# Another order of steps in a hybrid layer of gated DeltaNet and sparse attention

## The chip, the cores and the metric

The kernel runs on one core of one Trainium2 chip. The metric is the device time of one execution in microseconds (us). Before the change the median of three runs is 738.63 us (738.37 to 744.95).

## What is computed

One layer over 1024 tokens of 1024 numbers, in float32. A modulation of the input's root-mean-square norm gives `h`; one product `h @ w_in` (3792 columns) gives everything that follows, for two groups of heads. In outline:

```
h    = rmsnorm(x, g_pre) * (1 + scale) + shift           # shift, scale, gate from silu(c) @ w_ada
qkv, z_a, b, a, q_b, ckv, z_b, iq, ik, iw = split(h @ w_in)
# group A: 4 heads of 128, chunks of 64 tokens
q, k, v = silu(causal_conv(qkv, width 4)), q and k to length 1
T    = inverse(I + strict_lower((k beta) k^T decay))      # per head and chunk, 64 x 64
u, w = T (v beta), T (k beta exp(gc))
v'   = u - w S;  o = (q exp(gc)) S + ((q k^T) decay) v';  S = S exp(g_last) + k^T v'   # chunk after chunk
o_a  = rmsnorm(o, g_gdn) * silu(z_a)
# group B: 4 heads of 128 over a shared latent
score = sum over 8 index heads of iw * relu(iq ik^T), causal
sel   = the 256 highest scores of each query
o_b   = softmax(q_b ckv[sel]^T + bias) ckv[sel] w_uv * silu(z_b)
out  = x + gate * rmsnorm([o_a, o_b] @ w_out, g_post)
```

## The kernel before, in words

Products in float32 precision are made of three matmuls of split operands: the high part of a weight times both parts of `h`, and its low part times the high part of `h` (L430 to L432). A tile of 128 weight columns needs two halves of 24 such matmuls of 512 tokens each. Weight tiles come through a pipeline of one raw and two split buffers: each use (`nextw`) splits the next raw tile into `whi` (L174 or L176) and `wlo` (L181) and starts the load of the one after (L233, on SP's queue). The projections' results take turns in two PSUM banks, so the second next half waits until a half has been read.

What runs when comes from three tables. `PLAN` (L37) is a list of step names; each name is a generator that issues its instructions up to its next `yield`. `PARTS` says how many steps each has, and `ENGINES` (L59) puts single instructions on another engine than the usual one. A scheduler then orders what each engine gets, and weighs it by the steps' order. On the chip every engine takes its instructions in the order that results.

The steps which the change and the prediction speak of:

- `F`, `D0`, `D1`, `X`, `E`: first halves of projections, the input's norm and transposes, group A's decays' inputs.
- `I`, twelve steps: index queries, three steps for each of four weight tiles, and the scores of two heads each. A score is relu on ACT (L590), then either one DVE instruction (L189) or a multiply on ACT (L192) and an add on POOL (L193). The matmuls of scores are L579 and L580. `S`, twenty steps: the search for the 256th highest score bit by bit, by counts on ACT (L619) and DVE (L607); a round closes with L659 and L660.
- `K0`, `K1`: keys of a pair of heads with their convolutions (`conv_half`, L705; each tap is one `add_scaled`, L186 to L193), decay matrices (L537), and the stores of the matrices to invert (L850).
- `J0`, `J1`: the inverses' 32-wide blocks (`invert`). A load of `scr` (L861), a memset (L862), then thirty rounds of one multiply (L867) and one add (L869), all on POOL; a store (L871) and eight loads of `X` (L876).
- `M0`, `M1` (`merge`): transposes of `X` on DVE (L919, L920), then matmuls which put the blocks together. `R0`, `R1`: the recurrence. `Q`, `V`: queries and values with convolutions; `Z0`, `Z1`: group A's gates; `N`, `A`: its norm and mix.
- `HZ`, four steps: gates of group B. Each is one weight tile, silu on ACT (L1029) and a store (L1031). `HQ`: its queries (L1145 stores them).
- `C`: latents; `G`: the residual gate (its weights are loaded at L1055); `B`: biases; `W`: loads of `w_out`; `T0` to `T7`: attention of a block of 128 queries; `O0` to `O7`: the output product of a block.

The inverse's chain and its load and store:

```python
ns = blk((64, 32, 32), name="ns")
nc.sync.dma_start(flat(ns), scr[pr, 0])                 # L861
for i in range(30, 0, -1):
    G.tensor_tensor(tmp, ns[..i..], ns[..i+1..], op=ALU.mult)       # L867
    G.tensor_tensor(ns[..], ns[..], tmp, op=ALU.add)                # L869
    yield
nc.sync.dma_start(scr[pr, 1], flat(ns))                 # L871
```

`blk` takes the free buffer with the lowest number, so a step placed earlier may get another buffer, and waits for its last reader.

Of the kernel before, what the change touches and what calls it, by code (L numbers as in the profile page):

```python
# [36 lines left out]
PLAN = ("D0 F F X X X D1 F I F E I I K0 K0 I I I K0 I I K0 I I I I K0 HZ J0 J0 J0 J0 J0 J0 J0 J0 J0 J0 J0 J0 J0 "  # L37
# [4 lines left out]
        "O2 O7 O7 O5 O2").split()  # L42
# [7 lines left out]
for _p in range(8):  # L50
# [8 lines left out]
ENGINES = {"ad00": "V", "ad01": "V", "ad20": "V", "ad30": "V", "ad50": "V", "cT0": "V", "cT1": "V", "cv011": "A",  # L59
# [53 lines left out]
def hybrid_kernel(ctx, tc, x, c, w_ada, b_ada, g_pre, conv_w, a_log, dt_bias, g_gdn, g_kv, w_uv,  # L113
# [53 lines left out]
    def engine(site, usual, choice):  # L167
        SITES[site] = usual, choice
        return ENGINES.get(site, usual)

# [51 lines left out]
    readers = [1, 5]  # L222
    for n in PLAN:
        if done[n] in PARTS[n][1]:
# [1106 lines left out]
    step = dict.fromkeys(PARTS, 0)  # L1331
    outs = [n for n in PLAN if n[0] == "O"]
    for pos, n in enumerate(PLAN):
        if n == "B":
# [48 lines left out]
```

## Time and profile before

| | |
|---|---|
| median of three runs | 738.63 us |
| profiled execution | 746.19 us, span 744.5 us, mean granted TensorE clock 0.964 |
| TensorE matmul busy | 685.7 us (92%) |
| DVE / ACT / POOL busy | 529.7 / 436.9 / 336.3 us |
| DMA | 70.10 MB, mean 94 GB/s |

The granted clock is in shares of the full one. A matmul that waits shows in its row what released it, as `[0.57 <-DVE score L189]`: idle 0.57 us, ended by DVE's instruction that wrote `score` at line 189. SPq is SP's queue of DMA issues, `ps` a PSUM bank. Names like `ps` stand for many buffers.

### The profile page before, as it was taken

To read this page: it belongs to the slowest core of one execution; us is meant where nothing else is said; L and a number is where in the kernel's file an instruction comes from. 1 tells how busy PE (TensorE), PEld (TensorE's weight loads), DVE (VectorE), ACT (ScalarE), POOL (GpSimd) and SP (SyncE) were. 2 spreads that over 40 slices of the span, in tenths; PEclk is the share of its full clock that TensorE was granted. 3 is DMA by queue.
4 is the path that set the end of the run, shared out by engine and by line. 5 is a ranking of instruction groups with operands and counts; after the bars stand their busy time and mean duration, and the time that the engine had idled before them with its cause. 6 is when DMAs were issued, how large, how long until landed. Compare 5 with 4: busy or idle time off the path is not lost.

```text
span 744.5 us, 11292 instructions
## 1 busy us (share of the span) xinstructions
PE 685.7 (92%) x3863; PEld 574.7 (77%) x3863; DVE 529.7 (71%) x1342; ACT 436.9 (59%) x863; POOL 336.3 (45%) x395
## 2 busy tenths in 40 slices
PE   3999898999999899998998999988887999999996
PEld 2887787888778678876787878777765889888885
DVE  3977785663356866868689887877889999964212
ACT  4545584576668888859868494523336687434211
POOL 2146616456997300314432599941243232654310
PEclk9996999999999999999999999996799999999999
DMA  8931000013112111220032212276033205313311
GB/s 309 405 153 44 1 29 28 1 40 104 42 47 96 43 68 47 90 81 29 1 114 113 86 57 86 71 250 235 15 115 114 85 29 185 114 61 124 141 58 56
DMA packets 35287, 70.10 MB, mean 94 GB/s; under 512 B 11431, under 2 KB 18717, under 8 KB 35230
## 3 DMA queue, kind: packets, MB, share of 16 engines
q1 hardware_dynamic: 35230, 69.39, 26.5%
q8 instruction: 30, 0.49, 0.3%
q14 instruction: 27, 0.22, 0.1%
HBM read 53.64 MB, written 15.73 MB: 93 GB/s over the span
## 4 chain that ended last, share of the span: by engine, by line
PE 54%; DVE 16%; POOL 11%; DMA 6%; ACT 6%; issue 5%; SPq 1%; DVEq 0%; POOLq 0%; ACTq 0%
PE ps L430 8%; PE ps L432 8%; PE ps L431 8%; PE ps L1281 4%; PE ps L1279 4%; PE ps L1280 4%; POOL ns L869 4%; POOL rk L867 4%; ACT junk L619 2%; DVE pr L1217 1%; PE ps L1234 1%; DMA wraw<-in_w_tiles_dram 1%; DMA wa<-in_w_ada_dram 1%; DVE junk L607 1%; PE ps L579 1%
## 5 line engine op out<-in xcount | busy, mean ns | idle before, releaser
L430 PE MATMUL ps<-h,whi 128*128 128x512 f32 (+2 forms) x448 | 177.2, 396 | 12.8 <-DVE cv L189 6.7
L431 PE MATMUL ps<-h,whi 128*128 128x512 f32 (+2 forms) x448 | 177.0, 395 | 0.0
L432 PE MATMUL ps<-h,wlo 128*128 128x512 f32 (+2 forms) x448 | 176.0, 393 | 0.7 <-POOL wlo L181 0.7
L619 ACT ACTIVATE junk<-score,pat,sgn 128x1024 bf16<-128x1024 f32 (+2 forms) x93 | 105.5, 1135 | 11.5 <-DVE pat L660 10.3
L430 PEld LDWEIGHTS ps<-h,whi 128*128 128x128 f32 (+1 forms) x448 | 85.5, 191 | 34.2 <-DVE cv L189 7.8
L432 PEld LDWEIGHTS ps<-h,wlo 128*128 128x128 f32 (+1 forms) x448 | 85.4, 191 | 17.3 <-issue 0.9
L431 PEld LDWEIGHTS ps<-h,whi 128*128 128x128 f32 (+1 forms) x448 | 85.4, 191 | 15.9 <-issue 0.7
L607 DVE TENSOR_SCALAR_CACHE_REDUCE junk<-score,pat 128x640 bf16<-128x640 f32 (+2 forms) x93 | 68.8, 740 | 1.6
L193 POOL TENSOR_TENSOR cv<-cv,tmp 128x510 f32<-128x510 f32 (+2 forms) x33 | 39.1, 1186 | 42.6 <-ACT tmp L192 42.3
L1281 PE MATMUL ps<-woh,ml 128*128 128x512 f32 x128 | 49.9, 392 | 1.3 <-DVE ml L181 1.3
L590 ACT ACTIVATE ps<-ps 128x512 f32<-128x512 f32 (+3 forms) x70 | 34.1, 511 | 28.5 <-PE ps L580 27.9
L1280 PE MATMUL ps<-wol,mh 128*128 128x512 f32 x128 | 50.4, 394 | 0.0
L1279 PE MATMUL ps<-woh,mh 128*128 128x512 f32 x128 | 50.0, 393 | 0.0
L193 POOL TENSOR_TENSOR score<-score,tmp 128x512 f32<-128x512 f32 (+3 forms) x29 | 32.4, 1123 | 35.0 <-ACT tmp L192 30.7
L189 DVE SCALAR_TENSOR_TENSOR score<-ps,iw,score 128x384 f32<-128x384 f32 (+3 forms) x41 | 25.7, 643 | 28.1 <-ACT ps L590 22.8
L869 POOL TENSOR_TENSOR ns<-ns,rk 64x30 f32<-64x30 f32 (+14 forms) x60 | 36.1, 602 | 3.8
L181 POOL TENSOR_TENSOR wlo<-wraw,whi 128x1024 fp32r<-128x1024 f32 (+1 forms) x11 | 25.7, 2340 | 26.7 <-PE ps L432 19.9
L867 POOL TENSOR_TENSOR rk<-ns 64x30 f32<-64x30 f32 (+14 forms) x60 | 36.2, 604 | 3.2
L189 DVE SCALAR_TENSOR_TENSOR cv<-ps,cols,cv 128x511 f32<-128x511 f32 (+2 forms) x39 | 28.8, 738 | 6.2 <-POOL cv L193 4.3
L174 ACT ACTIVATE whi<-wraw 128x1024 fp32r<-128x1024 f32 x19 | 20.0, 1054 | 20.1 <-PE ps L431 12.7
L1283 ACT ACTIVATE junk<-ps 128x512 bf16<-128x512 f32 x16 | 9.5, 595 | 36.8 <-PE ps L1281 32.3
L181 DVE TENSOR_TENSOR wlo<-wraw,whi 128x1024 fp32r<-128x1024 f32 x19 | 24.7, 1299 | 8.7 <-ACT whi L174 7.8
(358 smaller groups left out, 1742.1 us busy)
## 6 DMA issues: line engine op xcount, KB each, us to landing
wraw<-in_w_tiles_dram SPq DMA_DIRECT2D x29, 512.0 KB, 3.5
wa<-in_ada_tiles_dram SPq DMA_DIRECT2D x16, 512.0 KB, 10.2
x<-in_x_dram SPq DMA_DIRECT2D x8, 512.0 KB, 3.3
qd<-qo SPq DMA_DIRECT2D x8, 512.0 KB, 3.0
wa<-in_w_ada_dram SPq DMA_DIRECT2D x8, 512.0 KB, 5.1
qb<-qd SPq DMA_DIRECT2D x8, 512.0 KB, 3.2
woraw<-in_w_out_dram SPq DMA_DIRECT2D x8, 512.0 KB, 3.4
xr<-in_x_dram SPq DMA_DIRECT2D x8, 512.0 KB, 3.9
```

Source lines behind the costliest of these rows:

```text
L189: V.scalar_tensor_tensor(o, a, scale, o, op0=ALU.mult, op1=ALU.add)
L193: G.tensor_tensor(o, o, tmp, op=ALU.add)
L430: mm(o, lhsT=hi[:, k, :], rhs=h[:, 0, c0:c1], start=(k == 0), stop=False)
L431: mm(o, lhsT=hi[:, k, :], rhs=h[:, 1, c0:c1], start=False, stop=False)
L432: mm(o, lhsT=lo[:, k, :], rhs=h[:, 0, c0:c1], start=False, stop=(k == NK - 1))
L607: V.tensor_scalar(junk[:, 0:src.shape[1]], src, t, None, op0=op, op1=ALU.add, accum_out=o)
L619: A.activation(junk[:, 0:(b + 1) * P], score[b], AF.Sign, scale=sg, bias=t, accum_out=o)
L867: G.tensor_tensor(tmp, ns[:, 0:i, i:i + 1].to_broadcast([64, i, w]), ns[:, i:i + 1, i + 1:32].to_broadcast([64, i, w]), op=ALU.mult)
L869: G.tensor_tensor(ns[:, 0:i, i + 1:32], ns[:, 0:i, i + 1:32], tmp, op=ALU.add)
L1279: mm(ps, lhsT=mh[:, k, :], rhs=woh[k][:, sl], start=(k == 0), stop=False)
L1280: mm(ps, lhsT=mh[:, k, :], rhs=wol[k][:, sl], start=False, stop=False)
L1281: mm(ps, lhsT=ml[:, k, :], rhs=woh[k][:, sl], start=False, stop=(k == NK - 1))
```

## The change

It replaces the two tables. `PLAN` is another order of the same 193 steps: the fourth index step, a query projection, comes ahead of the keys' first steps; the inverse J0 starts directly after K0, with the first search steps between, and group B's gates HZ come within it; values V0 come before group A's gates Z0; the second inverse begins ahead of HQ's last queries; Z1's last step lies between R1's steps; attention and output blocks have another order. `ENGINES` moves some eighty single instructions, among them nine score adds from ACT with POOL to DVE (`s161` to `s770`, gone from the table), three taps of convolutions, and casts of weights (`w...h`) and subtractions (`w...l`).

```diff
-PLAN = ("D0 F F X X X D1 F I F E I I K0 K0 I I I K0 I I K0 I I I I K0 HZ J0 J0 J0 J0 J0 J0 J0 J0 J0 J0 J0 J0 J0 "
-        "J0 J0 J0 Q0 HZ HZ S S S S Z0 V0 S V0 Z0 S S S M0 S Q0 M0 HZ HQ R0 R0 S R0 S R0 R0 R0 R0 R0 S K1 K1 N0 "
-        "N0 K1 S A0 K1 HQ K1 A0 S Q1 HQ V1 Q1 Z1 HQ J1 J1 J1 J1 J1 J1 J1 J1 V1 J1 J1 J1 J1 J1 J1 J1 J1 M1 M1 C "
-        "S S S S S S G R1 R1 R1 R1 C R1 R1 R1 Z1 B G R1 N1 N1 A1 A1 T6 T4 T7 T6 T7 T3 T6 W T0 T4 T5 T6 T7 T0 T4 "
-        "T3 W T5 T3 T1 T5 T2 T7 T4 T3 T0 O3 W T1 W W T1 T5 W W T1 O6 W O3 O4 T2 T0 O0 T2 T2 O6 O1 O4 O5 O0 O1 "
-        "O2 O7 O7 O5 O2").split()
+PLAN = ("F F X D0 X X D1 F I F E I I I K0 K0 I I I K0 I K0 I I I I K0 J0 J0 S S S S J0 S J0 J0 J0 Q0 HZ HZ J0 "
+        "J0 J0 J0 J0 J0 HZ J0 J0 V0 Z0 J0 V0 Z0 S J0 S M0 S Q0 M0 S HZ R0 R0 HQ S R0 S R0 R0 R0 R0 R0 S K1 K1 "
+        "N0 N0 A0 K1 A0 S K1 K1 HQ S S J1 Q1 J1 HQ V1 Q1 J1 J1 Z1 J1 J1 J1 J1 J1 J1 J1 J1 J1 HQ J1 S J1 J1 V1 "
+        "M1 M1 S S C S S R1 R1 R1 G Z1 R1 C R1 R1 G R1 B R1 N1 N1 A1 A1 T6 T7 T6 T7 T4 T3 T0 T6 W T4 T5 T6 T7 "
+        "T0 T4 T3 W T5 T3 T0 T1 T5 T2 T7 T4 T3 O3 W T1 W W T1 T5 W W T1 O1 W T0 O3 T2 T2 O0 O4 T2 O1 O0 O7 O6 "
+        "O6 O5 O7 O2 O4 O5 O2").split()
...
-           "pn710": "A", "qb00": "V", "qb01": "V", "qb03": "V", "qb10": "V", "qb12": "V", "qb13": "V", "qe0256":
-           "V", "qe0512": "V", "qe2256": "V", "qe3512": "V", "s150": "A", "s161": "A", "s171": "A", "s230": "A",
-           "s260": "A", "s330": "A", "s350": "A", "s370": "A", "s420": "A", "s430": "A", "s441": "A", "s471": "A",
-           "s530": "A", "s541": "A", "s550": "A", "s551": "A", "s560": "A", "s570": "A", "s630": "A", "s640": "A",
-           "s651": "A", "s660": "A", "s661": "A", "s720": "A", "s740": "A", "s750": "A", "s760": "A", "s761": "A",
-           "s770": "A", "se5": "G", "se9": "G", "sp0": "V", "sq000": "A", "sq001": "A", "sq010": "A", "sq011": "A",
...
+           "V", "qb12": "V", "qe0256": "V", "qe0512": "V", "qe2256": "V", "qe3512": "V", "s150": "A", "s171": "A",
+           "s230": "A", "s260": "A", "s330": "A", "s370": "A", "s420": "A", "s471": "A", "s530": "A", "s541": "A",
+           "s551": "A", "s560": "A", "s630": "A", "s660": "A", "s661": "A", "s720": "A", "s740": "A", "s750": "A",
+           "s760": "A", "s761": "A", "se0": "G", "se3": "G", "se5": "G", "se6": "G", "se8": "G", "se9": "G", "sp0":
+           "V", "sq000": "A", "sq001": "A", "sq010": "A", "sq011": "A", "sq101": "A", "sq110": "A", "sq111": "A",
...
```

What moves is seen in the order of the instructions on each engine; three places follow.

On TensorE, in the index phase. `ps<-khi,qe` and its like are score matmuls, `gm` decays, `h,whi` and `h,wlo` projections. Before:

```order
L580 MATMUL ps_1019<-klo_537,qe_823 128x320
L537 MATMUL ps_1048<-gm_1049,triSr 128x256 x2
L579 MATMUL ps_1023<-khi_536,qo_824 128x320
L580 MATMUL ps_1023<-klo_537,qo_824 128x320
L537 MATMUL ps_1048<-gm_1053,triSr 128x256 x2
L579 MATMUL ps_1028<-khi_536,qe_823 128x512
L580 MATMUL ps_1028<-klo_537,qe_823 128x512
L579 MATMUL ps_1032<-khi_536,qo_824 128x512
L580 MATMUL ps_1032<-klo_537,qo_824 128x512
L537 MATMUL ps_1059<-gm_1060,triSr 128x256 x2
```

The change:

```order
L580 MATMUL ps_1008<-klo_537,qe_823 128x320
L430 MATMUL ps_1305<-h_529,whi_1044 128x512
L431 MATMUL ps_1305<-h_529,whi_1044 128x512
L432 MATMUL ps_1305<-h_529,wlo_1045 128x512
L430 MATMUL ps_1305<-h_530,whi_1044 128x512
L579 MATMUL ps_1012<-khi_536,qo_824 128x320
L580 MATMUL ps_1012<-klo_537,qo_824 128x320
L579 MATMUL ps_1017<-khi_536,qe_823 128x320
L580 MATMUL ps_1017<-klo_537,qe_823 128x320
L537 MATMUL ps_1112<-gm_1113,triSr 128x256 x2
L431 MATMUL ps_1305<-h_530,whi_1044 128x512
L432 MATMUL ps_1305<-h_530,wlo_1045 128x512
```

The scores of the first pairs of heads and the decays stood without a projection between them; now the matmuls of one lie among them, three to nine at a time.

On SP's queue, around the first inverse. `scr<-X` stores what is to be inverted, `ns<-scr` is J0's load, `zd<-zo` a store of group B's gates. Before:

```order
L850 DMA scr<-X_1446 32x8x32 x4
L233 DMA wraw_1819<-in_w_tiles_dram 128x1024
L850 DMA scr<-X_1769 32x8x32 x4
L1031 DMA zd<-zo_1821 128x1024
L233 DMA wraw_2011<-in_w_tiles_dram 128x1024
L861 DMA ns_1875<-scr 64x1024
L1031 DMA zd<-zo_2013 128x1024
```

The change:

```order
L850 DMA scr<-X_1440 32x8x32 x4
L233 DMA wraw_2058<-in_w_tiles_dram 128x1024
L850 DMA scr<-X_1751 32x8x32 x4
L861 DMA ns_1797<-scr 64x1024
L1031 DMA zd<-zo_2060 128x1024
L233 DMA wraw_2118<-in_w_tiles_dram 128x1024
L1031 DMA zd<-zo_2120 128x1024
```

The load stands right behind the last store that it reads, where a gate's store and a weight load were ahead of it.

On DVE, at the first merge. `T<-X` are the transposes, `junk,cnt` counts of the search, `ok` the end of a round, `cv<-ps` a tap of a convolution whose reading frees a bank. Before:

```order
L189 SCALAR_TENSOR_TENSOR cv_2329<-ps_2336,cols,cv_2329 128x509
L660 SCALAR_TENSOR_TENSOR pat_2129<-ok_2131,thr_2130 128x6
L176 CAST whi_2460<-wraw_2334 128x1024
L607 TENSOR_SCALAR junk_2228,cnt_2127<-score_815,pat_2129 128x640
L658 TENSOR_SCALAR thr_2130<-pat_2129 128x6
L919 STREAM_TRANSPOSE T_2707<-X_1446 128x1024
L181 TENSOR_TENSOR wlo_2461<-wraw_2334,whi_2460 128x1024
L607 TENSOR_SCALAR junk_2230,cnt_2127<-score_816,pat_2129 128x512
L919 STREAM_TRANSPOSE T_2870<-X_1769 128x1024
L920 MEMSET T_2707 32x8x32
L607 TENSOR_SCALAR junk_2232,cnt_2127<-score_815,pat_2129 128x384
L178 TENSOR_SCALAR vn_2408<-ps_2409,gv_560 128x128
```

The change:

```order
L660 SCALAR_TENSOR_TENSOR pat_1811<-ok_1813,thr_1812 128x6
L607 TENSOR_SCALAR junk_1880,cnt_1809<-score_815,pat_1811 128x640
L658 TENSOR_SCALAR thr_1812<-pat_1811 128x6
L176 CAST whi_2364<-wraw_2273 128x1024
L919 STREAM_TRANSPOSE T_2657<-X_1440 128x1024
L607 TENSOR_SCALAR junk_1882,cnt_1809<-score_816,pat_1811 128x512
L181 TENSOR_TENSOR wlo_2365<-wraw_2273,whi_2364 128x1024
L919 STREAM_TRANSPOSE T_2820<-X_1751 128x1024
L920 MEMSET T_2657 32x8x32
L607 TENSOR_SCALAR junk_1884,cnt_1809<-score_815,pat_1811 128x384
L178 TENSOR_SCALAR vn_2345<-ps_2346,gv_560 128x128 x2
L189 SCALAR_TENSOR_TENSOR cv_2268<-ps_2310,cols,cv_2268 128x509
```

The transposes come two rounds of the search earlier, and the tap behind them is of the first value tile; Z0's first gate, which was ahead, is now behind that tile.

## Rows read from the trace of the kernel before

**Rows 1.** The page's first part: busy time and share of the span.

```profile
PE 685.7 (92%) x3863; PEld 574.7 (77%) x3863; DVE 529.7 (71%) x1342; ACT 436.9 (59%) x863; POOL 336.3 (45%) x395
```

**Rows 2.** Waits of TensorE by cause: us in total, times, longest us.

```profile
PE ps L430 <- DVE cv L189: 6.7, 3, 2.9
PE ps L1243 <- DVE pT L1238: 3.5, 1, 3.5
```

**Rows 3.** Timeline, TensorE in the index phase: start us, us, what, [idle before].

```profile
118.13 0.50 PE L579 MATMUL ps<-khi,qe 128*128 128x512 f32 x1 [0.57 <-DVE score L189]
...
122.06 0.50 PE L579 MATMUL ps<-khi,qe 128*128 128x512 f32 x1 [1.79 <-DVE qe L565]
```

**Rows 4.** Windows: length, busy us of PE, PEld, DVE, ACT, POOL, granted clock.

```profile
123.70:127.10 3.40, 3.40 (x10) 2.64 (x9) 1.98 (x3) 1.30 (x3) 1.30 (x2) 0.50 0.00 0
237.00:246.10 9.10, 9.10 (x41) 7.28 (x40) 5.86 (x18) 7.55 (x15) 3.77 (x11) 1.00 0.48 125
577.70:581.10 3.40, 3.19 (x15) 3.19 (x16) 3.35 (x11) 2.98 (x6) 0.00 (x0) 0.50 0.57 233
581.10:651.00 69.90, 67.66 (x476) 62.04 (x476) 66.15 (x213) 47.53 (x101) 26.73 (x17) 1.00 0.28 95
```

**Rows 5.** Waits of SP's queue at the load of `ns`: us, times, longest.

```profile
SPq L861 <- PE ps L432: 3.2, 1, 3.2
```

**Rows 6.** Timeline, SP's queue: the last stores of K0 and J0's load.

```profile
170.53 1.78 SPq L850 DMA_DIRECT2D scr<-X  x4
...
183.49 0.52 SPq L861 DMA_DIRECT2D ns<-scr  x1
```

**Rows 7.** DMA issues: count, KB each, median us from issue to landing.

```profile
scr<-X SPq DMA_DIRECT2D x16, 32.0 KB, 1.6
ns<-scr SPq DMA_DIRECT2D x2, 256.0 KB, 3.4
```

**Rows 8.** Timeline, POOL: begin, one round and end of J0's chain.

```profile
186.96 0.15 POOL L862 MEMSET ns<- 64x32 f32 x1 [0.22 <-DMA ns<-scr]
...
201.46 1.55 POOL L867 TENSOR_TENSOR rk<-ns 64x210 f32<-64x210 f32 x1
...
239.06 0.23 POOL L869 TENSOR_TENSOR ns<-ns,rk 64x30 f32<-64x30 f32 x1
```

**Rows 9.** Groups on POOL, 186.9 to 239.4: busy us, mean ns, idle before.

```profile
L867 POOL TENSOR_TENSOR rk<-ns 64x30 f32<-64x30 f32 (+14 forms) x30 | 16.5, 548 | 1.5
L869 POOL TENSOR_TENSOR ns<-ns,rk 64x30 f32<-64x30 f32 (+14 forms) x30 | 15.5, 516 | 1.8
L193 POOL TENSOR_TENSOR score<-score,tmp 128x448 f32<-128x448 f32 (+3 forms) x11 | 11.9, 1084 | 0.0
L181 POOL TENSOR_TENSOR wlo<-wraw,whi 128x1024 fp32r<-128x1024 f32 x1 | 2.4, 2405 | 1.0 <-ACT whi L174 1.0
```

**Rows 10.** Timeline, DVE: a weight subtraction, two round ends, the first merge.

```profile
201.23 1.35 DVE L181 TENSOR_TENSOR wlo<-wraw,whi 128x1024 fp32r<-128x1024 f32 x1 [0.87 <-PE ps L580]
...
231.91 0.17 DVE L659 TENSOR_TENSOR ok<-cnt,lim 128x6 int32<-128x6 f32 x1 [1.61 <-ACT junk L619]
...
242.92 0.17 DVE L659 TENSOR_TENSOR ok<-cnt,lim 128x6 int32<-128x6 f32 x1
...
246.10 1.25 DVE L919 STREAM_TRANSPOSE T<-X 128x1024 f32<-128x1024 f32 x1 [0.76 <-DMA X<-scr]
...
252.29 0.61 DVE L189 SCALAR_TENSOR_TENSOR cv<-ps,cols,cv 128x509 f32<-128x509 f32 x1
```

**Rows 11.** Timeline, TensorE at the first merge.

```profile
252.96 0.51 PE L430 MATMUL ps<-h,whi 128*128 128x512 f32 x1 [2.88 <-DVE cv L189]
```

**Rows 12.** The page's fifth part: groups of score adds, busy us, mean ns.

```profile
L193 POOL TENSOR_TENSOR score<-score,tmp 128x512 f32<-128x512 f32 (+3 forms) x29 | 32.4, 1123 | 35.0 <-ACT tmp L192 30.7
L189 DVE SCALAR_TENSOR_TENSOR score<-ps,iw,score 128x384 f32<-128x384 f32 (+3 forms) x41 | 25.7, 643 | 28.1 <-ACT ps L590 22.8
```

**Rows 13.** Waits of DVE at the transposes of `X`: us, times, longest.

```profile
DVE T L919 <- DMA X<-scr: 5.7, 2, 4.9
```

More of the change, by code (lines that the diff above doesn't have):

```diff
@@ L56 @@
 ADA = ((2, 2, 4), (1, 1, 2, 2, 2))
-ENGINES = {"ad00": "V", "ad01": "V", "ad20": "V", "ad30": "V", "ad50": "V", "cT0": "V", "cT1": "V", "cv011": "A",
[37 rows of a table removed]
+ENGINES = {"ad00": "V", "ad01": "V", "ad11": "V", "ad20": "V", "ad30": "V", "ad50": "V", "cT0": "V", "cT1": "V",
[37 rows of a table added]
 SITES = {}
```

63 rows, old and new, of the table ENGINES are left out of this document.

## The prediction

> **What bounds the kernel now.** The page's first part comes first [rows 1]: TensorE is busy 92% of the span, DVE 71%, POOL 45%. So no engine but TensorE can be the bound of the whole, and since TensorE's work is the same before and after, a new order can only win back time in which TensorE stands or runs at its lower clock, or lose some. Then TensorE's waits by cause [rows 2]: the largest sum is 6.7 us for a convolution add on DVE, with 2.9 us as its longest; one wait of 3.5 us is for attention's `pT`. Two more, in the index phase, are in the timeline [rows 3], and the place of the longest, in the first merge, in [rows 11]. Behind a stall the rows show a second cost: in 123.7 to 127.1 and in 577.7 to 581.1 TensorE is busy (nearly) throughout and its granted clock is 0.50 [rows 4], the lower of its two levels (1.2 against 2.4 GHz), and both stretches come just after waits [rows 2, 3]. In each, 3.4 us do the work of 1.7: 1.7 us lost. At the full clock a 512-column matmul takes 0.22 us of the engine's time (9.10 us hold 41 of them, [rows 4]), so 24 of them, half of one weight tile, take about 5.3 us, and 48 about 10.7.
>
> **How sums stand to the median.** Rows come from one execution of 746.19 us (span 744.5); the median of the runs shown is 738.63, 7.6 us less. I work out differences in the profiled execution and take them off the median.
>
> **Index phase.** The second index query projection now runs ahead of the last convolution of the key steps, so that 24 matmuls of that convolution, and some of the third tile, lie between score matmuls, where before scores and decays stood alone (first order piece). TensorE stood there 0.57 us for a score add on DVE and 1.79 us for the query [rows 3], and then lost 1.7 us to the clock. With about 5 us of projection in that stretch the waits are covered: 0.57 + 1.79 + 1.7 = **-4.1 us**. The cover is taken from later: score matmuls of the second and third query pair now meet 20 in a row with no projection between, where the longest such stretch was 12. No row shows it. Its bounds are nothing (score adds moved to DVE also free POOL) and the whole loss that the same thing shows now, 4.1 us. I take one gap of the mean size of the two, 2.36 / 2 = **+1.2 us**; it is nearer to these rows than to a longer run with a clock change, since nine score adds go from a POOL instruction of 1.12 us behind an ACT multiply to one DVE instruction of 0.64 [rows 12].
>
> **First inverse.** It is a chain of 60 small POOL instructions and it waits for one load. Before, that load was issued at 183.49, 13 us after the last of the stores it needs were being issued at 170.53 [rows 6]; ahead of it in SP's queue stood a gate's store and a weight load, and then the queue stood 3.2 us for a matmul of an index projection [rows 5], since the buffer had been that step's. The change issues the load straight behind those stores, ahead of group B's first gate store (second order piece), in a buffer that a step long done had used. The stores' issue ends at 172.3, they land 1.6 us later and the load takes 3.4 [rows 6, 7]: data at 177.3, where POOL's first instruction was at 186.96 [rows 8]. That is 9.7 us earlier. The chain does not stand alone on POOL: from 186.96 to 239.29 [rows 8] are 52.3 us, in which the rows show other work of 11.9 us (index adds) and 2.4 (a weight split) [rows 9], with smaller pieces 18.5 in all; 33.8 are the chain and its gaps. The new order puts 17.7 us of others inside it. One thing lengthens it. `rk` took 1.55 us at 201.46, where these take 0.55 on average [rows 8, 9]; beside it ran a DVE weight subtraction of 1.35 us from 201.23 [rows 10]. So such a subtraction costs the chain about 0.9 (the sizes here are a little above the average), and three instead of two lie beside it now. End: 177.3 + 33.8 + 17.7 + 0.9 = 229.7, against 239.29.
>
> A rule of the Trainium skill speaks against this part ("SBUF — State Buffer", section "SBUF: two separate sides"): DVE and GpSimd share one pair of ports, and a GpSimd instruction is shut out for the whole of a DVE instruction with two SBUF inputs. By the row the loss is 0.9 us of the 1.35; by the rule's full length it would be 1.4, the chain's end 230.2 and the forecast 0.5 us later.
>
> **First merge.** Before, from the chain's end at 239.29 to DVE's first transpose of `X` at 246.10 went 6.8 us (store, load) [rows 8, 10], and from there to TensorE's return at 252.96 another 6.9, because the convolution add that frees TensorE's bank stands behind both transposes on DVE (third order piece; 252.29 in [rows 10], wait in [rows 11]). The change makes two things earlier. X lands at 229.7 + 6.8 = 236.5. And on DVE the transposes stand two search rounds ahead of where they stood: behind the round that closed at 231.91, no longer behind 242.92 [rows 10]. From the later round's end to the transpose DVE took 246.10 - 0.76 - 242.92 = 2.4 us; the same from 231.91 is 234.3, so it stands 2.2 us for X, and the convolution add that waits behind is now that of group A's first value tile. TensorE comes back at 236.5 + 6.9 = 243.4, 9.6 us earlier, but has 48 matmuls less behind it (the second half of a gate and the first of a value tile), 10.7 us: **+1.1 us**, with a clock loss behind the stall as before. Bounds: DVE may find X waiting (return at 241.2: -1.1), or X comes at 239, with POOL waiting for late index adds (+3.6). Between them the worked-out end decides. Group B's gates themselves (24 matmuls a half) cost what they did, elsewhere; HQ's first queries keep their place.
>
> **Second inverse and merge.** DVE stands 4.9 us for the second X before its transpose [rows 13]. Three POOL adds of some 1.1 us [rows 12] leave the inside of this chain for one small one: about 2 us earlier. Against it, the residual gate's first weight loads now go onto SP around the same loads, and two of its DVE instructions stand ahead of the transposes, waiting for such a load; the latent projection can then stand for its bank. I take half of the 2 us, **-1.0**, bounds -2 and +2. The last group A gate moved into the second recurrence covers recurrence gaps that its second gate tile covered already: nothing; without it the cover is 24 matmuls, 5.3 us less.
>
> **Attention.** On DVE and TensorE block 4's first instructions move behind blocks 6 and 7, so that the 3.5 us wait [rows 2] and the half-clock 3.4 us after it [rows 4] could go: 5.2 us. But DVE was busy 3.35 of these 3.40 us and 66.15 of the 69.90 after them [rows 4]: it is the engine that TensorE waits for here, and a new order gives it no less work. Ends: 0 and -5.2; I take **-1.5**, nearer to the DVE row. What is late next is the same block 4. The changed order of output blocks lies in a stretch with TensorE fed throughout: nothing.
>
> Sum: -4.1 + 1.2 + 1.1 - 1.0 - 1.5 = -4.3: 738.63 - 4.3 = **734.3 us**; the profiled execution would have 741.9.
>
> **Rivals.**
> *Faster.* DVE has slack after all in attention: its 3.75 idle us of 69.90 [rows 4] stand late and take in the shift, so the whole 5.2 goes; the index phase has no new gap and X is there when DVE comes. -4.1 + 0 - 1.1 - 1.0 - 5.2 = -11.4: **727.2 us**. Against it is DVE's 3.35 of 3.40.
> *Slower.* The first X comes no earlier than before, because POOL takes its queue in order and the index adds in the middle of the chain wait for score matmuls, which come when TensorE gets to them, however early the load. DVE then stands at the first transpose from 234.3 to 246.1, with the search counts and the convolution add behind it, and TensorE returns at 252.96 with 10.7 us less done: -4.1 + 1.2 + 10.7 - 1.0 - 1.5 = +5.3, **743.9**, and 746.4 if the two small gains also fail, more if the longer stall brings a longer stretch at the low clock. For it: DVE did stand 4.9 us for the second X [rows 13]. Against: the groups that made up the first chain stood idle only 1.5 + 1.8 + 0.0 + 1.0 = 4.3 us in its 52 [rows 9]. It decides if X lands later than about 241 (236.5 + 4.3).
> *Nothing.* Waits are only passed on: the index gap returns at the third query tile and the rest cancels, -4.1 + 4.1 + 1.1 + 0 + 0: **739.7**.
>
> **Chances.** Forecast 0.54 (its own range 729 to 740), faster rival 0.20, slower 0.16, nothing 0.10. The range reaches to both: 726 to 745, leaving out the upper part of the slower rival and a little below the faster one, some 0.17. A measurement tells about 1% from no change: under 731.2 is faster, above 746.0 slower. Faster: a quarter of the forecast's 0.54 and nearly all of the faster rival's 0.20 = 0.33. Slower: over half of the slower rival's 0.16 with a little of the rest = 0.11. Within: 0.56.
>
> **What would show it.** Right: no wait over 0.5 us in the index scores around 118 and no clock of 0.5 behind it; the load of `ns` some 10 us earlier and its chain done near 227 in the new run; DVE idle some 2 us for X before its first transpose, TensorE idle some 6 us for the convolution add, then a low clock. Wrong: a gap with a low clock near the second index query tile; X landing after the time at which it did; a `pT` wait gone with no other in its place, or a recurrence with new waits, which I have at nothing.

## The result, and the profile after

The change runs in 733.77 us (median of four runs, 730.84 to 734.94); the kernel before, beside it on the same chip, in 741.35. The ratio is 0.9894 with a 95% interval of 0.9851 to 0.9938. In a second series it was 0.9873 (0.9840 to 0.9905). So the change is faster by 1.1 to 1.3%, where I had forecast 734.3 us and 0.6%. The kernel before has runs from 736 to 748 us on these chips, which is why its median was 738.63 in three runs and 740 to 742 in series of 17 to 29 runs.

The page's first part of the change shows less time on TensorE and ACT, and 5 us more on DVE [rows 1]:

```profile
PE 679.3 (93%) x3863; PEld 569.0 (78%) x3863; DVE 534.8 (73%) x1362; ACT 426.0 (58%) x838; POOL 332.9 (45%) x390
```

In its fifth part, the score adds on DVE and on POOL, which answer [rows 12]:

```profile
L189 DVE SCALAR_TENSOR_TENSOR score<-ps,iw,score 128x384 f32<-128x384 f32 (+3 forms) x50 | 31.8, 645 | 32.0 <-ACT ps L590 28.0
...
L193 POOL TENSOR_TENSOR score<-score,tmp 128x512 f32<-128x512 f32 (+3 forms) x20 | 22.7, 1136 | 32.6 <-ACT tmp L192 24.9
```

TensorE executes the same matmuls in all these kernels, so I compare them by its **loss**: for each matmul the time to the next one's start, less the usual time for its kind (the lower quartile over the run), summed. It holds waits and low clock together, and its differences agree with those of the spans: 744.5 - 733.1 = 11.4 us in the first two profiles, loss 12.6; 737.1 - 730.0 = 7.1 us in the second two, loss 7.6. The stretches end with the last matmul of the step named; all values are worked out from the matmuls' starts in each trace. Another way to take the quartile moves a column's sum by about 1 us, so differences of a few tenths mean nothing.

| loss in us, up to the end of | before | before, again | change | change, again |
|---|---|---|---|---|
| first index projection | 24.6 | 20.0 | 19.4 | 18.4 |
| decays of the first keys | 4.9 | 3.3 | 0.4 | 0.4 |
| first keys | 1.5 | 1.5 | 3.0 | 3.0 |
| third gate of group B | 5.2 | 5.2 | 3.8 | 3.8 |
| first values, first gates of group A | 6.8 | 4.6 | 2.6 | 2.9 |
| first recurrence | 15.4 | 15.5 | 16.5 | 16.5 |
| second queries, first of the second values | 4.8 | 6.6 | 3.7 | 3.7 |
| second merge | 15.1 | 14.8 | 15.2 | 16.7 |
| second recurrence | 15.2 | 13.5 | 12.3 | 11.6 |
| end | 13.9 | 14.1 | 17.8 | 14.6 |
| sum | 107.3 | 99.2 | 94.7 | 91.6 |

**Two profiles of one kernel differ by 8 us**, as the first two columns show, and most of it is clock: TensorE was busy 685.7 us in the one and 680.7 in the other with the same matmuls, and idle 2.4 us longer in the first. These windows are of the head of before, of before again, and of the index phase of before again (columns as in [rows 4]), each from its own profile:

```profile
58.80:72.50 13.70, 12.98 (x44) 9.78 (x45) 10.37 (x20) 6.97 (x13) 7.79 (x8) 0.50 0.17 57
```

```profile
55.70:62.50 6.80, 6.80 (x23) 4.94 (x23) 5.55 (x7) 3.59 (x7) 3.39 (x4) 0.50 0.15 42
...
117.00:124.00 7.00, 6.64 (x31) 5.55 (x32) 3.88 (x7) 2.15 (x4) 3.30 (x5) 1.00 0.23 75
```

The second of the two index waits, in the timeline of before again:

```profile
117.36 0.50 PE L579 MATMUL ps<-khi,qe 128*128 128x512 f32 x1 [1.80 <-DVE qe L565]
```

The same place of the same kernel had 13.7 us at half clock in one execution and 6.8 in another, and the half clock after the index waits [rows 4] did not come a second time, though the waits did ([rows 3] answered by 0.57 and 1.80 us). What is compared below is therefore the change again with before again, where not said otherwise. Of the 7.1 us between these two, TensorE was busy for 3.2 us less (677.5 against 680.7) and idle for 3.9 less: less clock loss and less waiting, in about equal parts.

**The index phase.** In the change's window there, TensorE has no gap and the full clock:

```profile
107.00:123.00 16.00, 16.00 (x85) 13.96 (x84) 12.18 (x21) 8.09 (x14) 9.11 (x10) 1.00 0.09 33
```

The two waits come back in smaller form near 150 us, where 24 scores now run bare, not the 20 that I had counted:

```profile
149.21 0.51 PE L579 MATMUL ps<-khi,qo 128*128 128x512 f32 x1 [0.64 <-DVE score L189]
...
151.43 0.39 PE L430 MATMUL ps<-h,whi 128*128 128x256 f32 x1 [0.55 <-ACT tmp L192]
```

**The first inverse and merge.** The change's timeline of SP's queue, answering [rows 6]:

```profile
163.62 1.78 SPq L850 DMA_DIRECT2D scr<-X  x4
166.83 0.52 SPq L861 DMA_DIRECT2D ns<-scr  x1
182.17 0.34 SPq L1031 DMA_DIRECT2D zd<-zo  x1
```

of POOL, answering [rows 8]:

```profile
170.14 0.15 POOL L862 MEMSET ns<- 64x32 f32 x1 [2.25 <-DMA ns<-scr]
...
197.34 1.52 POOL L869 TENSOR_TENSOR ns<-ns,rk 64x240 f32<-64x240 f32 x1
...
199.62 0.70 POOL L869 TENSOR_TENSOR ns<-ns,rk 64x240 f32<-64x240 f32 x1
...
221.23 0.23 POOL L869 TENSOR_TENSOR ns<-ns,rk 64x30 f32<-64x30 f32 x1
```

of DVE, answering [rows 10]:

```profile
196.98 1.36 DVE L181 TENSOR_TENSOR wlo<-wraw,whi 128x1024 fp32r<-128x1024 f32 x1
...
224.47 0.15 DVE L659 TENSOR_TENSOR ok<-cnt,lim 128x6 int32<-128x6 f32 x1
...
227.65 1.25 DVE L919 STREAM_TRANSPOSE T<-X 128x1024 f32<-128x1024 f32 x1 [1.22 <-DMA X<-scr]
...
233.53 0.72 DVE L189 SCALAR_TENSOR_TENSOR cv<-ps,cols,cv 128x509 f32<-128x509 f32 x1
```

and of TensorE, answering [rows 11]:

```profile
232.03 0.50 PE L430 MATMUL ps<-h,whi 128*128 128x512 f32 x1 [0.69 <-ACT zo L1029]
...
249.58 0.50 PE L430 MATMUL ps<-h,whi 128*128 128x512 f32 x1 [0.46 <-ACT tmp L192]
```

From the stores to the chain's first instruction it is 6.5 us, where it was 16.4; the load is issued 15 us ahead of the gate's store that it used to wait behind. DVE stands 1.22 us for X. But the convolution add that I had put in TensorE's way starts at 233.53, and TensorE was back at 232.03, released by the silu of group A's first gate on ACT: it never waited for that add. Its next wait for a bank, at 249.58, is 0.46 us behind a tap on ACT.

### The profile page after: what moved, and what is told of

The parts are those of the page before. It is cut to its first block, busy times and chain, and to the rows that moved or that the text cites. A ratio compares the mean times of both kernels' runs of the same rounds, so it can differ in the third digit from the quotient of the medians.

```text
span 733.1 us, 11303 instructions
## 1 busy us (share of the span) xinstructions
PE 679.3 (93%) x3863; PEld 569.0 (78%) x3863; DVE 534.8 (73%) x1362; ACT 426.0 (58%) x838; POOL 332.9 (45%) x390
## 4 chain that ended last, share of the span: by engine, by line
PE 53%; DVE 15%; POOL 11%; ACT 7%; DMA 7%; issue 5%; SPq 1%; DVEq 0%; POOLq 0%; ACTq 0%
PE ps L430 6%; PE ps L431 6%; PE ps L432 6%; POOL ns L869 4%; POOL rk L867 4%; PE ps L1280 4%; PE ps L1281 4%; PE ps L1279 4%; ACT junk L619 2%; PE ps L1234 2%; DMA wa<-in_w_ada_dram 1%; DVE junk L607 1%; PE ps L580 1%; PE ps L579 1%; POOL cv L193 1%
## 5 line engine op out<-in xcount | busy, mean ns | idle before, releaser
L430 PE MATMUL ps<-h,whi 128*128 128x512 f32 (+2 forms) x448 | 175.4, 392 | 9.4 <-ACT zo L1029 2.6
L431 PE MATMUL ps<-h,whi 128*128 128x512 f32 (+2 forms) x448 | 174.5, 390 | 0.0
L432 PE MATMUL ps<-h,wlo 128*128 128x512 f32 (+2 forms) x448 | 173.5, 387 | 0.5 <-POOL wlo L181 0.5
L430 PEld LDWEIGHTS ps<-h,whi 128*128 128x128 f32 (+1 forms) x448 | 84.1, 188 | 30.0 <-ACT tmp L192 4.9
L431 PEld LDWEIGHTS ps<-h,whi 128*128 128x128 f32 (+1 forms) x448 | 84.3, 188 | 15.5 <-issue 0.4
L189 DVE SCALAR_TENSOR_TENSOR score<-ps,iw,score 128x384 f32<-128x384 f32 (+3 forms) x50 | 31.8, 645 | 32.0 <-ACT ps L590 28.0
L193 POOL TENSOR_TENSOR cv<-cv,tmp 128x509 f32<-128x509 f32 (+2 forms) x30 | 37.3, 1243 | 36.6 <-ACT tmp L192 36.3
L193 POOL TENSOR_TENSOR score<-score,tmp 128x512 f32<-128x512 f32 (+3 forms) x20 | 22.7, 1136 | 32.6 <-ACT tmp L192 24.9
L181 POOL TENSOR_TENSOR wlo<-wraw,whi 128x1024 fp32r<-128x1024 f32 (+1 forms) x10 | 23.5, 2346 | 30.3 <-issue 10.2
L189 DVE SCALAR_TENSOR_TENSOR cv<-ps,cols,cv 128x511 f32<-128x511 f32 (+2 forms) x42 | 31.2, 743 | 5.7 <-POOL cv L193 4.0
L181 POOL TENSOR_TENSOR wol<-woraw,woh 128x1024 fp32r<-128x1024 f32 x8 | 19.5, 2447 | 27.9 <-ACT woh L174 24.3
L534 POOL TENSOR_TENSOR gm<-triU,gdp 128x512 fp32r<-128x512 f32 x16 | 16.5, 1045 | 30.9 <-PE ps L537 22.5
```

What stands on the lines that cost most here:

```text
L189: V.scalar_tensor_tensor(o, a, scale, o, op0=ALU.mult, op1=ALU.add)
L193: G.tensor_tensor(o, o, tmp, op=ALU.add)
L430: mm(o, lhsT=hi[:, k, :], rhs=h[:, 0, c0:c1], start=(k == 0), stop=False)
L431: mm(o, lhsT=hi[:, k, :], rhs=h[:, 1, c0:c1], start=False, stop=False)
L432: mm(o, lhsT=lo[:, k, :], rhs=h[:, 0, c0:c1], start=False, stop=(k == NK - 1))
```

## The experiments

All variants change the two tables alone. Ratios are against before on the same chip. A step that is put back also makes the scheduler order other instructions anew: in the index step's run ACT's and DVE's orders differ from the change's from the index phase to the first merge. So most of these runs move more than the step that they name.

**The change again, and before again.**

> The change as it is, beside its variants on the same chip. Both theories: about 0.989 of the kernel before. If the 13.7 us of half clock near 58.8 us in the profile of before and the 3.4 us in that of the change belong to the kernels (theory: the order of the first steps), the next profile of the change shows 3.4 us again; if they are chance (rival), it can show either.

> The kernel before, unchanged, for a second profile of it. Theory (the long half clock of 13.7 us in its head belongs to a wait of 0.72 us at 59.62 and is there in some executions only): another length there, 3.4 to 7 us, and 3 to 5 us less excess before the first index step; the rest of the profile as it was. Rival (it is the kernel's own): 13.7 us again.

The change: 0.9873 (0.9840 to 0.9905); half clock in its head 3.4 us again. Before: 738.79 us in its one run, half clock 6.8 us in the head, its loss there 4.6 us less. So half-clock length in the head is no property of the kernel before. Nor is it one of the change: runs below with the change's head had 6.8 us there (the early load, the gate and block 4 among them). In the first profile the stretch begins at 58.80, ahead of the wait at 59.62 that I had named as its source; what starts it stays open.

**The head's order put back.**

```diff
-PLAN = ("F F X D0 X X D1 ...
+PLAN = ("D0 F F X X X D1 ...
```

> The change with its first six steps in the order of before; on TensorE four single-column products move behind two matmuls, nothing else moves. Theory (the head's difference is chance): the change's time, 0.988 of before, half clock in the head of 3.4 to 7 us. Rival (this order makes the long half clock): some 4 us slower, 13.7 us of half clock from about 58 us.

0.9885 (0.9823 to 0.9947): no difference from the change. Its loss up to the first index projection was 17.3 us against 18.4, with 6.8 us at half clock. The head's order is worth nothing measurable; that all variants lie at 17 to 20 us there and before at 20.0 and 24.6 is not explained by it, and stays open.

**The index step put back.**

```diff
-... I F E I I I K0 K0 I I I K0 ...
+... I F E I I K0 K0 I I I I K0 ...
```

> The change with its fourth index step put back behind the keys' second step, as before. Theory (cover by projections in the index phase, worth 4.5 us around 118 us and costing 1.4 later): about 3 us slower than the change, 0.993 of before, with waits and a half-clock stretch again near 118 to 124 us. Rival (the gain comes from the nine score adds that left POOL, not from the order): the same time as the change, no waits there.

1.0020 (1.0000 to 1.0039): not 3 but 11 us slower than the change, the whole gain gone. Up to the first keys it went the way I expected, but by less: loss 2.7 in place of 0.4 and 1.8 in place of 3.0, which is 1.1 us in all and not 3, and no half clock came near 118 us. The rest came later: 6.2 in place of 3.8 up to group B's third gate, 8.0 in place of 2.9 up to the first gates of group A, where one wait stands out. TensorE's row in this kernel's timeline, and then ACT's before it:

```profile
255.75 0.79 PE L430 MATMUL ps<-h,whi 128*128 128x512 f32 x1 [4.14 <-ACT tmp L192]
```

```profile
251.95 1.24 ACT L619 ACTIVATE junk<-score,pat,sgn 128x1024 bf16<-128x1024 f32 x1 [0.82 <-DVE pat L660]
...
253.32 1.13 ACT L619 ACTIVATE junk<-score,pat,sgn 128x896 bf16<-128x896 f32 x1
...
255.02 1.25 ACT L192 ACTIVATE tmp<-ps,cols 128x509 f32<-128x509 f32 x2
```

and ACT's in the change again, where TensorE waits 0.74 us at this place:

```profile
247.01 1.03 ACT L619 ACTIVATE junk<-score,pat,sgn 128x768 bf16<-128x768 f32 x1
...
248.19 0.69 ACT L192 ACTIVATE tmp<-ps,cols 128x509 f32<-128x509 f32 x1
248.77 1.23 ACT L619 ACTIVATE junk<-score,pat,sgn 128x1024 bf16<-128x1024 f32 x1
```

The tap of the second value tile (`tmp`, 509 wide), which frees TensorE's bank, stands ahead of the next search round's counts in the change, and behind two of them here; and that round waits for DVE to close the one before. The rows show the tap's place and the wait for it; no run moves that tap by itself, so that its place is the cause is argued and not shown. The rival is out: with the score adds still on DVE, a wait of 1.50 us on an index query came back at 117 us.

**The early load taken back.**

```diff
-... K0 J0 J0 S S S S J0 S J0 J0 J0 Q0 HZ HZ J0 ...
+... K0 HZ J0 J0 S S S S J0 S J0 J0 J0 Q0 HZ J0 ...
```

> The change with group B's first gate step put back ahead of the first inverse: the load of ns again behind a gate's store and a weight load. Theory (the early load is what took the stall out of the first merge): the chain ends about 8 us later, TensorE waits 3 to 4 us at the first merge, 3 to 4 us slower than the change, 0.994 of before. Rival (the value tile ahead of the gate did it, by another bank): the chain ends later too, but TensorE waits under 1 us and the time is the change's.

0.9952 (0.9928 to 0.9977): 4 to 6 us slower than the change. SP issues the load at 175.50, 14 us behind the stores, and the first merge has two waits with a half-clock stretch behind each; loss there 9.5 in place of 2.9. In its timeline, SP's load and TensorE's two waits:

```profile
175.50 0.51 SPq L861 DMA_DIRECT2D ns<-scr  x1
```

```profile
231.06 0.47 PE L430 MATMUL ps<-h,whi 128*128 128x512 f32 x1 [2.21 <-DVE cv L189]
...
252.88 0.79 PE L430 MATMUL ps<-h,whi 128*128 128x512 f32 x1 [3.14 <-ACT tmp L192]
```

The first is the same matmul as the change's at 232.03, but here it waits for the add on DVE, because its half of the gate got another bank. That add stands ahead of both transposes here, so this wait is not one for X. X is late at the second: the round of the search closes on DVE behind the second transpose, ACT stands 4.75 us for it, and the tap of the second value tile comes behind the counts of the rounds that follow. DVE's add and transposes, and ACT's count:

```profile
230.17 0.75 DVE L189 SCALAR_TENSOR_TENSOR cv<-ps,cols,cv 128x509 f32<-128x509 f32 x1
...
234.12 1.25 DVE L919 STREAM_TRANSPOSE T<-X 128x1024 f32<-128x1024 f32 x1 [1.89 <-DMA X<-scr]
...
237.25 1.25 DVE L919 STREAM_TRANSPOSE T<-X 128x1024 f32<-128x1024 f32 x1 [1.49 <-DMA X<-scr]
```

```profile
238.63 1.24 ACT L619 ACTIVATE junk<-score,pat,sgn 128x1024 bf16<-128x1024 f32 x1 [4.75 <-DVE pat L660]
```

The edit moved the load and, with the gate step, the bank. The time lies near the theory's, but only the second wait can be the load's, and no run has the late load with the change's bank: how much of the 4 to 6 us is the load's stays open.

**The gate put back ahead of the value tile.**

```diff
-... HZ J0 J0 V0 Z0 J0 V0 Z0 ...
+... HZ J0 J0 Z0 V0 J0 V0 Z0 ...
```

> The change with group A's first gate put back ahead of its first value tile. Theory (early load): X is there in time whatever comes first, no wait above 1.5 us, the time within 1 us of the change. Rival (the value tile's taps must be ahead of the transposes on DVE and the gate's second half covers them): TensorE waits 3 us or more at the first merge, about 3 us slower than the change.

0.9911 (0.9883 to 0.9939) against 0.9873, or 0.9894 in the change's first series: 1 to 3 us slower by the middle values, but the intervals overlap and the difference is not clear of noise. In the profile the loss at the first merge is 5.7 in place of 2.9; some 2 us less at the second merge make up for most of it. X is there as early, and the longest wait is for an add that comes late on DVE, in the timelines of DVE and of TensorE:

```profile
242.98 0.74 DVE L189 SCALAR_TENSOR_TENSOR cv<-ps,cols,cv 128x509 f32<-128x509 f32 x1
```

```profile
243.77 0.50 PE L430 MATMUL ps<-h,whi 128*128 128x512 f32 x1 [1.89 <-DVE cv L189]
```

Neither theory nor rival holds as stated: the longest wait, 1.89 us, lies between what the two said. The order of gate and value tile had a part of it. With the value tile first, its taps come sooner, and a gate, whose bank ACT frees, lies behind it.

**The tail's order put back**, attention and output in the order of before behind the change's front.

```diff
-... A1 A1 T6 T7 T6 T7 T4 T3 T0 T6 W T4 ... O6 O6 O5 O7 O2 O4 O5 O2
+... A1 A1 T6 T4 T7 T6 T7 T3 T6 W T0 T4 ... O0 O1 O2 O7 O7 O5 O2
```

> The change with attention and output blocks in the order of before. Theory (attention is bound by DVE there, so that its order passes waits on): within 1.5 us of the change, 0.988 of before. Rival one (my forecast's term): 1.5 us slower. Rival two (the changed order costs the 1.9 us wait at 625.34 in its first profile and its half clock): 3 us faster than the change.

0.9923 (0.9892 to 0.9953): some 2 to 4 us slower than the change, at the edge of what the intervals tell apart. That is nearest to rival one; rival two is out. The early blocks lose less, and later ones more, with a half-clock stretch that the change again hasn't; two rows of TensorE's timeline, and the window behind them (columns as in [rows 4]):

```profile
613.32 0.39 PE L1243 MATMUL ps<-pT,cnh 128*128 128x256 f32 x1 [1.83 <-DVE pT L1238]
616.10 0.58 PE L1241 MATMUL ps<-pT,cnh 128*128 128x256 f32 x1 [1.96 <-DVE pT L176]
```

```profile
614.40:621.20 6.80, 5.10 (x16) 4.42 (x17) 5.12 (x15) 3.48 (x9) 2.74 (x2) 0.50 0.14 54
```

**Block 4 early**, the one move of that order which fills the longest wait of the change's attention.

```diff
-... T6 T7 T6 T7 T4 T3 T0 T6 W ...
+... T6 T4 T7 T6 T7 T3 T0 T6 W ...
```

> The change with block 4's first attention step put back behind block 6's first, as before; its 12 matmuls stand on TensorE where the change waits 3.4 us between block 7's first and group A's norm. Theory (that wait is a gap of order, and DVE pays nothing for the earlier logits): waits before group A's norm 1.5 to 2 us shorter, 1.5 us faster than the change, 0.986 of before. Rival (attention is bound by DVE, so the wait moves to the next blocks): the same time as the change, another wait of 1.5 us or more at 560 to 580 us.

0.9888 (0.9849 to 0.9927): the change's time. The wait of 3.27 us on DVE's `vn` in the change is 1.12 here (the change's row, then this kernel's); in its place there is one of 3.13 at block 6's last step, with half clock behind it. TensorE's timelines, and this kernel's windows between the two waits and behind the second (columns as in [rows 4]):

```profile
555.66 1.30 PE L1018 MATMUL ps<-ident,vn 128*128 128x128 f32 x8 [3.27 <-DVE vn L1015]
```

```profile
552.35 1.26 PE L1018 MATMUL ps<-ident,vn 128*128 128x128 f32 x8 [1.12 <-DVE vn L1015]
...
583.78 0.58 PE L1241 MATMUL ps<-pT,cnh 128*128 128x256 f32 x1 [3.13 <-ACT pT L174]
```

```profile
553.00:581.00 28.00, 24.24 (x161) 21.61 (x160) 25.18 (x84) 18.14 (x35) 9.52 (x5) 0.94 0.21 76
581.70:588.50 6.80, 4.72 (x13) 3.85 (x14) 3.19 (x10) 3.33 (x6) 2.22 (x1) 0.50 0.01 2
```

In the 28 us between them DVE was busy 25.18. The rival holds, though its wait came a little later than it said: the wait was passed on.

**A key step put back between the index steps.**

```diff
-... K0 K0 I I I K0 I K0 ...
+... K0 K0 I I K0 I I K0 ...
```

> The change with the keys' third step put back ahead of the seventh index step; the longest stretch of score matmuls without a projection is 14 in place of 24. Theory (the 1.5 us of gaps near 150 us come from that stretch): these gaps go, 1.5 us faster than the change if nothing else moves. Rival (the order up to the first merge is balanced so closely that any move of a step costs a round of the search there): gaps near 150 us go, but 3 us or more of new waits between 200 and 260 us, slower than the change.

0.9959 (0.9929 to 0.9989): 6 us slower than the change. The waits near 150 us are still there in pieces (0.40, 0.38 and 0.56), and the tap's wait is back:

```profile
150.08 0.39 PE L430 MATMUL ps<-h,whi 128*128 128x256 f32 x1 [0.56 <-ACT tmp L192]
...
253.74 0.80 PE L430 MATMUL ps<-h,whi 128*128 128x512 f32 x1 [4.00 <-ACT tmp L192]
```

Splitting the bare stretch brings nothing, and the rival holds for the new wait, not for the gaps near 150 us.

**Order alone, table alone.** The changed `PLAN` with the `ENGINES` of before, and the reverse.

> The changed order of steps with the engine table of before. Theory (the order carries the gain, the table was fitted to it and carries little): 0.990 of before, the index phase as in the change. Rival (nine score adds off POOL and the moved casts are what let the chain end in time): the first chain ends 5 us or more later than in the change, waits of 3 us or more at the first merge, 0.996 or more of before.

> The order of before with the changed engine table. Theory (order and table fit only together: the order alone came out at 1.004 of before): no faster than before, 0.998 to 1.008. Rival (the table carries most of the gain): 0.992 or less.

Order alone: 1.0037 (1.0010 to 1.0063). Table alone: 1.0101 (1.0069 to 1.0133). Both: 0.9873. Each half makes the kernel slower, and together they make it faster: 0.4% and 1.0% would have added up to 1.4% slower. So the theory of the order alone falls, and the table alone came out even slower than its theory's range. The order alone does fill the index phase (loss 0.4 up to the decays), but loses 6.1 up to group B's third gate, 6.1 at the first merge and 19.4 at the second (change: 3.8, 2.9, 16.7). The table alone loses 8.1 at the first merge and 21.0 in attention.

**Order with the nine score adds of the table.**

```diff
-... "s150": "A", "s161": "A", "s171": "A", ... "s350": "A", ... "s430": "A", "s441": "A", ...
-... "s550": "A", ... "s570": "A", ... "s640": "A", "s651": "A", ... "s770": "A", ...
+... "s150": "A", "s171": "A", ...
```

> The changed order with the engine table of before, in which only the nine score adds of the change go to DVE. Theory (they are the table's part that lets the first chain and the scores end in time; the order alone lost 6 us between the end of the keys and the first merge against the change): stalls up to the first merge as in the change, 6 us faster than the order alone, 0.996 of before; the rest of the table is worth the 5 us that remain, at the second merge. Rival (the table is fitted as a whole): within 2 us of the order alone, 1.003 of before.

1.0022 (0.9991 to 1.0054): no better than the order alone. Here is POOL's group of score adds within the chain, of the order alone and then of this kernel, and two waits of TensorE in this kernel's timeline:

```profile
L193 POOL TENSOR_TENSOR score<-score,tmp 128x320 f32<-128x320 f32 (+3 forms) x16 | 17.2, 1077 | 0.0
```

```profile
L193 POOL TENSOR_TENSOR score<-score,tmp 128x448 f32<-128x448 f32 (+3 forms) x11 | 11.9, 1078 | 0.0
```

```profile
228.40 0.47 PE L430 MATMUL ps<-h,whi 128*128 128x512 f32 x1 [3.23 <-DVE cv L189]
...
254.60 0.80 PE L430 MATMUL ps<-h,whi 128*128 128x512 f32 x1 [3.05 <-ACT tmp L192]
```

The adds do what I thought they do: five of them less within the chain, 5.3 us less, and DVE's first transpose starts at 226.38 where it was 234.70. TensorE has nothing from it: it waits for taps on DVE and on ACT, as the two rows show. My theory of this run falls, and the rival holds: these nine adds alone do not bring the order's gain. Which of the other entries do, no run shows.

No variant beat the change.

One wait runs through five of the slower variants. The matmul that opens group A's second gate waits for a bank that the second value tile's tap on ACT frees. In the change that wait is 0.46 and 0.74 us, and 0.36 to 0.85 in the runs that alter only the head or the tail. It is 4.14 with the index step back, 3.14 with the early load back, 4.00 with the key step back, 2.64 with the order alone and 3.05 with the order and the adds, and in each of the five traces 3.4 or 6.8 us at half clock begin within 1.9 us of its end. That tap's place among the search's counts is the likeliest common cause; it was not varied alone.

## Why the forecast was right, and where it was not

The direction was right, and the time (734.3 against 733.77) by luck: I took 4.3 us off a median of 738.63, while the change took 7.6 us off one of 741.35, and the two errors cancel. The gain was larger than forecast, 7.6 us of loss between the second profiles and 7.6 us between the medians of the first series against 4.3, and it lay partly elsewhere.

- **Index phase, -4.1.** Right in mechanism: 3.3 to 0.4, which is -2.9; -4.5 between the first profiles. The waits of 2.4 us went in both; the 1.7 us of clock behind them are in one profile of before only. Taking the step back brings one of the waits back.
- **The bare scores, +1.2.** Right in sign and size: 1.5 to 3.0, with waits of 0.64 and 0.55 in the rows; the bare stretch has 24 score matmuls, where I had counted 20, and splitting it did not take the waits out.
- **The first inverse.** Right: I had its data 9.7 us earlier; from stores to chain it is 6.5 in place of 16.4, 9.9 less. The chain with all that lies in it lasts 51.3 us, from 170.14 to 221.46, against my 52.4: one weight subtraction fewer lies beside it than I had counted. One that does cost what I had taken from the row of before, or a little less: POOL's instruction at 197.34 took 1.52 us, where the next of its line and shape took 0.70, beside a DVE subtraction of 1.36 from 196.98: 0.8 for 0.9. By the Trainium skill ("SBUF — State Buffer", section "SBUF: two separate sides"), whichever of a GpSimd instruction and a DVE instruction with two SBUF inputs starts first has the shared ports for its whole length, and the other is blocked. This trace nearly agrees: POOL's instruction began 0.36 us into the subtraction, 1.00 us of which was left, and 0.82 were lost. In the rows of before 1.12 were left and about 0.9 lost, so that my forecast was wrong to hold the loss against the subtraction's full length.
- **The first merge, +1.1.** Wrong, in sign: 5.2 to 3.8 and 4.6 to 2.9 in the two stretches, -3.1. The step that failed is "TensorE comes back at 236.5 + 6.9 = 243.4": I let the gate's second half wait for the bank of the value tile's last add. It got the bank that the gate's own first half had freed, on ACT, and its 24 matmuls (5.3 us, 232.03 to 237.31) covered the rest of DVE's way to that add at 233.53. What I counted as less work behind it was cover. DVE's wait was right in kind, 1.2 us against 2.2. Taking the early load back puts 6.6 us of loss into this stretch, part of it by another bank, and the old order of gate and value tile 2.8.
- **Second inverse and merge, -1.0.** Not found: 14.8 to 16.7, and 15.1 to 15.2 in the first profiles. DVE's wait of 4.9 us for the second X [rows 13] is gone in the change, and with it a wait of TensorE behind the transposes. But TensorE has a longer one in the change, for group B's last queries on DVE, which now lie inside the second inverse; a tap's wait is there in both, 1.65 us before, 0.85 and 2.11 in the change. The two waits for DVE, before and then in the change:

```profile
492.35 0.50 PE L430 MATMUL ps<-h,whi 128*128 128x512 f32 x1 [1.25 <-DVE cT L176]
```

```profile
461.07 0.74 PE L430 MATMUL ps<-h,whi 128*128 128x512 f32 x1 [2.53 <-DVE qo L1144]
```

  What I left out is the price of those queries there. The residual gate's loads release none of these waits.
- **Recurrences and the stretch between, nothing.** The second recurrence went from 13.5 to 11.6 and the second queries with the first of the values from 6.6 to 3.7: -4.8, of which I had none. The first recurrence lost 1.0. Between the first profiles it is -2.9 and -1.1; the second queries' 6.6 holds 3.4 us at half clock that the first profile of before has not. By the same count the second recurrence loses about 12.5 with the order alone and 14.1 with the table alone, the second queries' stretch about 5.2 and 3.9. That points to the order for the one and to the table for the other; which steps or entries do it, no run shows.
- **Attention, -1.5.** Not found: 14.1 to 14.6, and 13.9 to 17.8 in the first profiles. The `pT` wait [rows 2] did go, and there is one of 3.27 us for `vn` ahead of it; block 4 early passes that on in its turn. That DVE is the bound there was the right reason, and should have brought the term to nothing. Behind the change's front the old order is some 3 us slower, so far as the intervals tell, so this term cannot be read without the front.
- **The head, nothing.** Loss 20.0 to 18.4; its order is worth nothing measurable.

Of the rivals, the slower one's condition was not met: the transpose that waited for X started at 227.65, 64.0 us after the stores' issue at 163.62, where it took 75.6 before. The faster one's gain of 11.4 is about as far above the measured 7.6 as my 4.3 is below it, and its way was not the one taken: attention gave nothing. I had not thought of the rival that decides most: that order and table pay only together.

## What to carry to other kernels

A planned order and a table of engines are one plan: either half of this change alone made the kernel 0.4 to 1.0% slower, and taking back a single step cost up to all of the gain, up to 140 us downstream of the step. Before a stall behind an engine's queue is priced, read which buffer the waiting instruction gets and whose reading frees it; work whose buffer another engine frees can cover the stall. Where losses are waits with a low clock behind them, take two profiles of the kernel before, since the clock's part comes in one execution and not in the next.

## What was not expected of the hardware

The length of a half-clock stretch at one place of an unchanged kernel was 13.7 us in one execution and 6.8 in the other, and 3.4 us or none after the same two waits in the index phase. The waits themselves agreed to 0.01 us (0.57 and 0.57, 1.79 and 1.80).
